# Moving the start of the weights inside their buffers: gate, up, down and the feature-major mixer units of a hybrid decoder trunk

## The chip, the cores and the metric

The kernel runs on one core of a Trainium2 chip. The metric is the device time of one execution in microseconds; each kernel is run several times and the median counts. TensorE (PE in the profile) multiplies, VectorE (DVE), ScalarE (ACT) and GpSimd (POOL) do the element-wise work, SyncE (SP) issues the loads. SBUF is the on-chip memory of 128 partitions; an address here is a byte within a partition, the same in all 128. A matmul of TensorE has two operands in SBUF: the stationary one, up to 128 x 128 numbers, which a weight load (PEld) puts into the array, and the moving one, whose columns stream through.

## What is computed

Two layers, each a half-step SwiGLU FFN, three token mixers side by side and another half-step FFN; then a final RMSNorm. 512 tokens, width 1024, FFN width 2816, everything float32.

```
for l in range(DEPTH):
    h = rms_norm(x, ffn1_norm[l])
    x = x + 0.5 * (silu(h @ wg1[l]) * (h @ wu1[l])) @ wd1[l]
    h = rms_norm(x, mix_norm[l])
    parts = split(h @ w_in[l])            # 4616 columns
    mixed = concat(hgrn2(parts), gated_deltanet(parts), retention(parts))
    x = x + mixed @ w_out[l]
    h = rms_norm(x, ffn2_norm[l])
    x = x + 0.5 * (silu(h @ wg2[l]) * (h @ wu2[l])) @ wd2[l]
return rms_norm(x, final_norm)
```

## The kernel before

**Numbers as hi and lo.** [...] To keep precision each operand is split into a rounded part hi and the rest lo, and a product is the sum of three: hi·hi, hi·lo, lo·hi (`mm3`, L217). The activations are held transposed, feature by token: eight tiles of 128 features by 512 tokens for `xh` and eight for `xl`; after the gate, `ah` and `al` per 128 columns of the FFN width.

**A unit of weights.** A unit is a block of 128 output columns with all its rows: for gate, up and the feature-major mixer columns 8 blocks of 128 x 128 (1024 numbers in a partition), for down 8 or 6 blocks. `load` (L194) brings raw weights by a DMA on SP's queue, 256 columns at a time, into one of two `raw` buffers. `split` makes the unit: ACT copies it to a `hi` tile with rounding, then DVE (or POOL, in the mixer at listed turns) subtracts to make `lo`. `unit` gives the tiles: each is a buffer of UNIT = 1088 numbers (4352 bytes, 17 x 256) in a pool of four for hi and a pool of four for lo, and the unit is laid in it from element `at` on:

```
t = pool.tile([P, UNIT], F32R, tag=tag, name=tag)
return t[:, at:at + shape[1] * shape[2]].rearrange("p (k f) -> p k f", k=shape[1])
```

`at` is 0 unless it is given. It is NARROW = 16 elements (64 bytes) in two places: the token-major mixer units, where the weights are the moving operand of 256 or 264 columns (`ps_tm`), and the last down group of the kernel, which runs in two halves of 256 tokens (`end`). Everything else begins at byte 0 of its buffer.

**Where buffers lie.** In this program's allocation the xh and xl tiles begin at byte 23296 and follow each other at 2048 bytes, the hi buffers at byte 72448 and the lo buffers at byte 89856, each 4352 bytes after the one before; the tiles that hold ah and al begin at 115456 and are 2048 apart. All of these are multiples of 256. A small pad tile (PAD = 56 elements) stands ahead of xh. A 128 x 128 block of a unit begins 512 bytes after the one before.

**The FFN.** `ffn` walks three groups of 8, 8 and 6 column blocks. For each block it runs 24 matmuls for gate (`pg`) and 24 for up (`pu`), each with a stationary 128 x 128 block of weights and 512 moving columns of `xh` or `xl`; then, after a group, eight down units (`pd`), 24 or 18 matmuls each, with `ah` or `al` moving. So gate and up take turns every 24 matmuls, and a down group is 192 or 144 matmuls long. Weights are split one unit or more ahead; the four buffers of a pool set how far. The first gate unit of the kernel is built apart, in `run`, and also begins at byte 0.

**The mixer.** `stream_units` makes the units in the order of a written plan; `dense_stream` runs the dense products and `interleave` puts the small matmuls of the mixer chains between them. Feature-major units (`ps_fm`, L260) have the weights stationary and 512 tokens moving, 24 matmuls each, as in the FFN. The output projection (`ps_out`) also streams 512 columns, from units that begin at byte 0.

Between two matmuls with different stationary blocks stands a weight load, and here every matmul has one of its own. The next load runs beside the current matmul.

Of the kernel before, what the change touches and what calls it, by code (L numbers as in the profile page):

```python
# [19 lines left out]
P = 128  # L20
D = 1024
KD = D // P
# [76 lines left out]
PAD = 56  # L99

NARROW = 16
STEP = 1600
SLICE = 2200
LAT = 1.4
# [61 lines left out]
class Kern:  # L166
# [63 lines left out]
    def stream_units(self, plan, w_out):  # L230

        for kind, cols, _ in plan:
            if kind == "fm":
                (c0, n), = cols
                raw = self.load([self.w_in[:, c0:c0 + n]], KD)
                for j in range(0, n, P):
                    yield self.split(raw[:, :, j:j + P], [P, KD, P])
            else:
                n = sum(w for _, w in cols)
                for k0 in (0, 4):  # L240
                    raw = self.load([self.w_in[:, c:c + w] for c, w in cols], 4, k0)
                    yield self.split(raw, [P, 4, n], NARROW)
        for groups in OUT_PARTS:
            n = 512 // len(groups)
            for c0 in range(0, D, n):
                raw = self.wraw.tile([P, 2 * len(groups), n], F32, tag="raw", name="raw")
                for i, g in enumerate(groups):
                    r = GROUP[g] * 256
                    self.nc.sync.dma_start(raw[:, 2 * i:2 * i + 2, :],
                                           w_out[r:r + 256, c0:c0 + n].rearrange("(k p) f -> p k f", p=P))  # L250
                yield self.split(raw, [P, 2 * len(groups), n])
# [190 lines left out]

    def gate_up(self, wg, wu, group, narrow=0, begin=(0, 0)):
        f0, nf = GROUPS[group]
        return [self.dense_units(w[:, f0 * P:(f0 + nf) * P], KD, narrow, b) for w, b in zip((wg, wu), begin)]

    def ffn(self, wg, wu, wd, layer, norm, meanwhile=None, begun=None):
        nc = self.nc
        xs = list(self.xs)
        for gi, (f0, nf) in enumerate(GROUPS):  # L450
            act, queue = [], deque()
            gu, uu = self.gate_up(wg, wu, gi) if gi or not begun else begun

            hold = 0 if gi else 2 if begun else 1
            for f in range(nf):
                where = lambda i: (self.pb, "b") if 3 <= 2 * f + i <= 2 * hold + 1 else (self.pa, "a")
                pool, tag = where(0)
                pg = pool.tile([P, T], F32, tag=tag, name="pg")
                self.mm3(pg, next(gu), xs, KD)
                if hold and f == hold:  # L460
                    self.stats_rows()
                    while queue:
                        queue.popleft()()
                pool, tag = where(1)
                pu = pool.tile([P, T], F32, tag=tag, name="pu")
                self.mm3(pu, next(uu), xs, KD)
                if hold and f == 0:
                    self.stats_tok()
                queue.append(lambda pg=pg, pu=pu: act.append(self.gated(pg, pu)))
                if f >= hold:  # L470
                    queue.popleft()()
            if gi == 0 and meanwhile:
                with self.tc.issue_after(self.last_load.ins):
                    meanwhile()
            last = gi == len(GROUPS) - 1
            if last and layer == DEPTH:
                return self.end(lambda: self.dense_units(wd[f0 * P:(f0 + nf) * P, :], nf, at=NARROW), act, nf)
            for d, dw in enumerate(self.dense_units(wd[f0 * P:(f0 + nf) * P, :], nf)):
                pd = self.pb.tile([P, T], F32, tag="b", name="pd")
                self.mm3(pd, dw, act, nf)  # L480
                nc.vector.scalar_tensor_tensor(self.x[d], pd, 0.5, self.x[d], ALU.mult, ALU.add)
                if last:
                    self.prepare(d, self.sv[layer][norm])
# [824 lines left out]
    def interleave(self, dense, waiting):  # L1308
# [3 lines left out]
        while more or any(waiting.values()) or running:  # L1312
# [5 lines left out]
            if r and (r[0] <= self.pe or not more):  # L1318
                self.pe = max(self.pe, r[0])
                self.done = self.pe  # L1320
                with self.tc.high_priority(offset=PRIO[r[1]]):
                    if next(r[2], self) is self:
                        running.remove(r)
                r[0] = max(self.done * LAT + self.pe * (1 - LAT), self.pe) + STEP
                continue
# [199 lines left out]
```

## Time and profile before

| | |
|---|---|
| median of 3 runs | 2191.91 us (2185.59 to 2193.06) |
| profiled execution | 2192.0 us, span 2190.2 us |
| TensorE busy | 2154.9 us, 98% of the span |
| weight loads busy | 1829.6 us, 84% |
| VectorE, ScalarE, GpSimd busy | 52%, 38%, 23% |
| mean granted TensorE clock | 0.992 |
| DMA | 203 MB, 93 GB/s |

Each line of the profile is the work of one core in one execution. A matmul's own duration includes its way through the array, which overlaps the next one, so the time that it costs is read from one start to the next. The chain of waits goes back from the last instruction, at each step to what released it.

### The profile page before, as it was taken

To read this page: it belongs to the slowest core of one execution; us is meant where nothing else is said; L and a number is where in the kernel's file an instruction comes from. 1 tells how busy PE (TensorE), PEld (TensorE's weight loads), DVE (VectorE), ACT (ScalarE), POOL (GpSimd) and SP (SyncE) were. 2 spreads that over 40 slices of the span, in tenths; PEclk is the share of its full clock that TensorE was granted. 3 is DMA by queue.
4 is the path that set the end of the run, shared out by engine and by line. 5 is a ranking of instruction groups with operands and counts; after the bars stand their busy time and mean duration, and the time that the engine had idled before them with its cause. 6 is when DMAs were issued, how large, how long until landed. Compare 5 with 4: busy or idle time off the path is not lost.

```text
span 2190.2 us, 31776 instructions
## 1 busy us (share of the span) xinstructions
PE 2154.9 (98%) x13079; PEld 1829.6 (84%) x13079; DVE 1147.9 (52%) x1980; ACT 842.4 (38%) x1319; POOL 500.4 (23%) x466
## 2 busy tenths in 40 slices
PE   8999999998999999999999999999899999999998
PEld 7888888887988788888888888888889888888888
DVE  5544345468497743433543343364866876434335
ACT  5322224555555422222432222254654544222225
POOL 2201013454333210101211010133633412101011
PEclk9999999999999999999999999999999999999999
DMA  4323234221123323232232322242121232323223
GB/s 155 126 78 116 77 106 140 73 78 40 59 60 106 97 97 96 78 115 80 94 116 96 97 97 96 82 148 79 59 59 40 73 103 88 104 94 99 96 87 126
DMA packets 197757, 203.08 MB, mean 93 GB/s; under 512 B 7626, under 2 KB 189292, under 8 KB 197612
## 3 DMA queue, kind: packets, MB, share of 16 engines
q1 hardware_dynamic: 197612, 201.05, 29.0%
q8 instruction: 103, 1.69, 0.3%
q14 instruction: 42, 0.34, 0.0%
HBM read 194.74 MB, written 6.29 MB: 92 GB/s over the span
## 4 chain that ended last, share of the span: by engine, by line
PE 86%; DVE 9%; ACT 2%; issue 1%; POOL 0%; DMA 0%; SPq 0%; DVEq 0%; ACTq 0%; POOLq 0%
PE pd L217 22%; PE pu L217 22%; PE pg L217 22%; PE ps_fm L260 7%; PE ps_tm L260 5%; PE ps_out L260 2%; DVE aw L149 1%; PE ps_scan L265 1%; DVE lo L149 1%; PE ps_ss L265 1%; DVE blk_p L149 1%; DVE x L149 1%; PE ps_ao L265 1%; DVE flo L149 1%; PE ps_al L265 0%
## 5 line engine op out<-in xcount | busy, mean ns | idle before, releaser
L149 ACT CAST hi<-raw 128x1024 fp32r<-128x1024 f32 (+2 forms) x369 | 379.2, 1028 | 1094.2 <-PE pg L217 323.0
L149 DVE TENSOR_TENSOR lo<-raw,hi 128x1024 fp32r<-128x1024 f32 (+2 forms) x325 | 390.2, 1201 | 80.9 <-ACT hi L149 68.5
L149 POOL TENSOR_TENSOR g<-g,rstd 128x512 f32<-128x512 f32 x88 | 150.2, 1706 | 1130.2 <-ACT g L146 1130.2
L217 PE MATMUL pd<-ah,hi 128*128 128x512 f32 (+1 forms) x752 | 282.0, 375 | 0.0
L217 PE MATMUL pd<-ah,lo 128*128 128x512 f32 (+1 forms) x752 | 281.6, 375 | 0.0
L217 PE MATMUL pd<-al,hi 128*128 128x512 f32 (+1 forms) x752 | 281.6, 375 | 0.0
L217 PE MATMUL pg<-xl,hi 128*128 128x512 f32 x704 | 275.0, 391 | 1.0 <-DVE xl L149 1.0
L217 PE MATMUL pu<-xh,hi 128*128 128x512 f32 x704 | 274.4, 390 | 0.6 <-ACT hi L149 0.6
L217 PE MATMUL pg<-xh,hi 128*128 128x512 f32 x704 | 274.5, 390 | 0.1
L217 PE MATMUL pg<-xh,lo 128*128 128x512 f32 x704 | 274.2, 389 | 0.0
L217 PE MATMUL pu<-xh,lo 128*128 128x512 f32 x704 | 274.1, 389 | 0.0
L217 PE MATMUL pu<-xl,hi 128*128 128x512 f32 x704 | 273.9, 389 | 0.0
L149 DVE TENSOR_TENSOR u<-pu,g 128x512 f32<-128x512 f32 x88 | 60.9, 692 | 280.7 <-PE pu L217 265.2
L149 DVE SCALAR_TENSOR_TENSOR x<-pd,x 128x512 f32<-128x512 f32 (+1 forms) x104 | 67.4, 649 | 229.3 <-PE pd L217 229.0
L149 DVE TENSOR_TENSOR g<-pg,rstd 128x512 f32<-128x512 f32 x88 | 60.8, 691 | 206.8 <-PE pg L217 206.7
L217 PEld LDWEIGHTS pd<-al,hi 128*128 128x128 f32 x752 | 141.4, 188 | 25.7
L217 PEld LDWEIGHTS pd<-ah,lo 128*128 128x128 f32 x752 | 141.3, 188 | 25.4
L217 PEld LDWEIGHTS pd<-ah,hi 128*128 128x128 f32 x752 | 141.1, 188 | 25.5
L217 PEld LDWEIGHTS pg<-xl,hi 128*128 128x128 f32 x704 | 132.3, 188 | 29.3 <-DVE xl L149 2.1
L217 PEld LDWEIGHTS pg<-xh,hi 128*128 128x128 f32 x704 | 132.5, 188 | 27.8 <-ACT xh L149 0.4
L217 PEld LDWEIGHTS pu<-xh,hi 128*128 128x128 f32 x704 | 132.1, 188 | 28.2 <-ACT hi L149 1.0
L217 PEld LDWEIGHTS pu<-xh,lo 128*128 128x128 f32 x704 | 132.3, 188 | 27.5
(331 smaller groups left out, 3778.5 us busy)
## 6 DMA issues: line engine op xcount, KB each, us to landing
raw<-in_ffn_w_gate_dram SPq DMA_DIRECT2D x43, 1024.0 KB, 5.1
raw<-in_ffn_w_up_dram SPq DMA_DIRECT2D x43, 1024.0 KB, 5.1
raw<-in_ffn_w_down_dram SPq DMA_DIRECT2D x32, 1024.0 KB, 4.7
raw<-in_w_in_dram SPq DMA_DIRECT2D x20, 1024.0 KB, 5.2
raw<-in_w_in_dram SPq DMA_DIRECT2D x32, 512.0 KB, 3.6
raw<-in_ffn_w_down_dram SPq DMA_DIRECT2D x20, 768.0 KB, 4.4
xd<-x SPq DMA_DIRECT2D x16, 256.0 KB, 2.5
raw<-in_w_out_dram SPq DMA_DIRECT2D x16, 256.0 KB, 2.6
```

What stands on the lines that cost most here:

```text
L149: return f(*args, **kw)
L217: self.nc.tensor.matmul(ps, a[:, k, :], b, start=n == 0, stop=n == 3 * nk - 1)
L260: self.nc.tensor.matmul(ps, a, b, start=start, stop=stop)
L265: self.nc.tensor.matmul(ps, a, b, start=start, stop=stop)
```

## The change

A table gives each kind of unit a start of its own, in elements of 4 bytes: gate 60, up 44, down 36, and the feature-major mixer units 28, that is 240, 176, 144 and 112 bytes. `gate_up`, `ffn` and `stream_units` pass it on to `dense_units` and `split`, and so to `unit`. Sizes of tiles and pools, loads, engines, the order of the work and the number of instructions stay. The token-major units, the last down group of the kernel, the output projection's units and the very first gate unit keep their starts. What moves is the address that ACT, DVE and POOL write, that DVE and POOL read hi from, and that TensorE loads the weights from.

```diff
+WIDE = {"gate": 60, "up": 44, "down": 36, "mix": 28}
...
                 raw = self.load([self.w_in[:, c0:c0 + n]], KD)
                 for j in range(0, n, P):
-                    yield self.split(raw[:, :, j:j + P], [P, KD, P])
+                    yield self.split(raw[:, :, j:j + P], [P, KD, P], WIDE["mix"])
...
     def gate_up(self, wg, wu, group, narrow=0, begin=(0, 0)):
         f0, nf = GROUPS[group]
-        return [self.dense_units(w[:, f0 * P:(f0 + nf) * P], KD, narrow, b) for w, b in zip((wg, wu), begin)]
+        return [self.dense_units(w[:, f0 * P:(f0 + nf) * P], KD, narrow, b, WIDE[n])
+                for w, b, n in zip((wg, wu), begin, ("gate", "up"))]
...
-            for d, dw in enumerate(self.dense_units(wd[f0 * P:(f0 + nf) * P, :], nf)):
+            for d, dw in enumerate(self.dense_units(wd[f0 * P:(f0 + nf) * P, :], nf, at=WIDE["down"])):
```

## The prediction

> **What bounds the kernel now.** First the page: busy time by engine, and the chain that ended last.
>
> ```profile
> span 2190.2 us, 31776 instructions
> PE 2154.9 (98%) x13079; PEld 1829.6 (84%) x13079; DVE 1147.9 (52%) x1980; ACT 842.4 (38%) x1319; POOL 500.4 (23%) x466
> ...
> PE pd L217 22%; PE pu L217 22%; PE pg L217 22%; PE ps_fm L260 7%; PE ps_tm L260 5%; PE ps_out L260 2%; DVE aw L149 1%; PE ps_scan L265 1%; DVE lo L149 1%; PE ps_ss L265 1%; DVE blk_p L149 1%; DVE x L149 1%; PE ps_ao L265 1%; DVE flo L149 1%; PE ps_al L265 0%
> ```
>
> TensorE carries the chain: the three FFN products take two thirds of it, the feature-major mixer product `ps_fm` 7%. The next view is the chain in order of time (start, length, what), then the busy time of each engine in a gate/up stage and in a down stage (length; busy time and count of PE, PEld, DVE, ACT, POOL; granted clock; DMA share; GB/s).
>
> ```profile
> 48.71 5.44 PE pg L217 x24
> 54.15 5.44 PE pu L217 x24
> ...
> 234.18 43.52 PE pd L217 x192
> ...
> 342.98 32.64 PE pd L217 x144
> ```
> ```profile
> 147.14:234.18 87.04, 87.04 (x385) 72.07 (x385) 34.80 (x39) 26.32 (x33) 13.90 (x8) 1.00 0.32 103
> 234.18:277.70 43.52, 43.52 (x193) 36.04 (x193) 15.94 (x17) 9.03 (x10) 0.00 (x0) 1.00 0.26 86
> ```
>
> The reader is to see a rigid beat. A unit of 24 matmuls takes 5.44 us, 192 take 43.52 and 144 take 32.64: each time 226.67 ns from one start to the next, at a granted clock of 1.00, with no wait between units. Only something that changes this beat can move the FFNs, because weights arrive early (DVE is 40% busy, ACT 30%, DMA 32%).
>
> How many matmuls does the edit touch? The groups by form of TensorE, one of three alike for each product (hi·hi, hi·lo, lo·hi), and one weight load:
>
> ```profile
> L217 PE MATMUL pg<-xh,hi 128*128 128x512 f32 x704 | 274.5, 390 | 0.1
> L217 PE MATMUL pu<-xl,hi 128*128 128x512 f32 x704 | 273.9, 389 | 0.0
> L217 PE MATMUL pd<-al,hi 128*128 128x512 f32 x656 | 254.7, 389 | 0.0
> L260 PE MATMUL ps_fm<-xl,hi 128*128 128x512 f32 x320 | 128.8, 403 | 0.0
> L260 PE MATMUL ps_out<-mh,lo 128*128 128x512 f32 x128 | 50.5, 394 | 0.0
> L217 PE MATMUL pd<-al,hi 128*128 128x256 f32 x96 | 26.9, 281 | 0.0
> L217 PEld LDWEIGHTS pg<-xh,lo 128*128 128x128 f32 x704 | 132.3, 188 | 27.0
> ```
>
> A matmul's own duration (389 ns) is longer than the beat because consecutive ones overlap; I use start-to-start times alone. Touched are 3 x 704 for gate less the first unit's 24 (it is built apart and keeps byte 0), 3 x 704 for up, 3 x 656 for down: 2088 + 2112 + 1968 = 6168 in the FFNs; and 3 x 320 = 960 `ps_fm`. `ps_out` stays at byte 0, the 256-wide down product stays at 64 bytes. All touched weights are the stationary operand of a 512-column stream; the streamed operand does not move.
>
> **The change part by part.** It adds and removes no instruction, no wait, no DMA and no buffer; it moves where ACT and DVE (or POOL) write a unit's hi and lo and where TensorE loads them from.
>
> *Writers.* No tile of the trace begins off a 64-byte step, so the nearest rows are the casts of 768 columns: at byte 0 (first row, a window around the first last-group of down) and at byte 64 (second row, a window at the end of the kernel):
>
> ```profile
> L149 ACT CAST hi<-raw 128x768 fp32r<-128x768 f32 x5 | 4.2, 840 | 12.1 <-PE pd L217 7.2 <-PE pu L217 3.8 <-ACT xh L149 0.9
> ```
> ```profile
> L149 ACT CAST hi<-raw 128x768 fp32r<-128x768 f32 x13 | 10.7, 830 | 10.8 <-PE pu L217 3.8 <-PE pd L217 3.6 <-DMA raw<-in_ffn_w_down_dram 3.3
> ```
>
> 840 and 830 ns: no penalty. I take zero; were a cast a tenth longer, ACT would still be under 35% busy in the stage above. The cover is the 5.44 us that TensorE spends on the unit before; gone, each ns would count once per unit.
>
> *TensorE.* 512 columns cost 226.67 ns. Is that the stream alone, or does the weight load that runs beside it hold it up? The trace has two witnesses. First, the 256-wide token-major product (`ps_tm`), as a timeline (start, length, instruction) in two stretches of the same line, operand tiles and start offsets, and ahead of it the busy times there (TensorE first; the granted clock is the third number from the end).
>
> ```profile
> 472.00:490.00 18.00, 15.58 (x129) 13.91 (x131) 17.59 (x40) 9.92 (x17) 11.79 (x19) 1.00 0.19 60
> ...
> 652.00:653.50 1.50, 1.50 (x15) 1.50 (x15) 1.47 (x3) 1.38 (x3) 0.31 (x1) 1.00 0.43 146
> ```
> ```profile
> 471.96 0.28 PE L260 MATMUL ps_tm<-hi,xh 128*128 128x256 f32 x1
> ...
> 476.20 0.28 PE L260 MATMUL ps_tm<-hi,xh 128*128 128x256 f32 x1
> ```
> ```profile
> 652.06 0.28 PE L260 MATMUL ps_tm<-hi,xh 128*128 128x256 f32 x1
> ...
> 654.22 0.28 PE L260 MATMUL ps_tm<-hi,xl 128*128 128x256 f32 x1
> ```
>
> The clock is 1.00 in both. The first stretch makes 36 steps in 4.24 us, 117.8 ns each; the second 19 steps in 2.16 us, 113.7 ns. One instruction form has two beats, 4.1 ns apart, and each holds until something interrupts it. Second witness, the wide product after an interruption (the 0.5 us of `ps_ms` ahead of it):
>
> ```profile
> 31.26 0.40 PE L217 MATMUL pu<-xh,hi 128*128 128x512 f32 x1
> ...
> 33.34 0.39 PE L217 MATMUL pu<-xh,hi 128*128 128x512 f32 x1
> ...
> 36.74 0.39 PE L217 MATMUL pg<-xh,hi 128*128 128x512 f32 x1
> ```
>
> Nine steps in 2.08 us are 231.1 ns each; the next fifteen in 3.40 us are 226.7. So the step depends on how the stream and the load beside it stand to each other in time, and it settles. I read this as two readers of the same memory that sometimes want the same part of it. If so, the place where the weights begin relative to the stream (both at multiples of 256 bytes today) is a second way to set that relation, and the edit turns it by 240, 176, 144 or 112 bytes, all odd multiples of 16, which no row shows.
>
> The price per wide matmul is therefore bounded from both sides. Best: the whole excess goes. The slower narrow beat and the wide one differ by 226.67 - 117.8 = 108.9 ns for 256 columns, so 512 columns with no fixed part would take 217.7 ns, 9.0 below today. Worst: the unsettled 231.1 ns stays, 4.4 above. Between them I take the one step that the trace shows between two settled beats of one form, 4.1 ns down, since a shifted start is most like a shifted phase.
>
> The rule in the Trainium skill that speaks against this is in "TensorE: Matmul & The Clock Gate", section "Step-by-step: what each phase is for": the stream and LDWEIGHTS have independent SBUF read ports, and loading the next weights doesn't take bandwidth from the running matmul. By it the sum would be zero and the time 2192; it does not account for 113.7 beside 117.8. The same page's section "Wait — 56ns, not 53.3ns?" gives 215.7 ns for back-to-back matmuls of 512 columns; by that figure 11 ns per matmul could go at most, an estimate of 2114 us.
>
> *The sum.* FFNs: every touched matmul is on the chain, 6168 x 4.1 = 25.3 us. `ps_fm`: 960 x 226.67 = 218 us of streaming, of which the chain holds 7% of 2190 = 153 us, so 70% of 960 x 4.1 = 3.9 counts, 2.8 us. Together 28 us. The profiled execution took 2192.0 us with a span of 2190.2, and the median of the runs shown is 2191.91, the same within 0.1 us: 2192 - 28 = **2164 us**. What is late next? Nothing: at 222.6 ns a unit takes 5.34 us, against some 2.2 us of DVE per unit (34.80 / 16).
>
> **The rivals.**
>
> *The beat is the stream's own.* 226.67 ns is what 512 columns of this type cost, and the load has room beside it (188 of 227 ns). For it: no gap in 192 matmuls, and hi and lo in all eight weight buffers, against xh, xl, ah and al, give one beat. It also settles from an interruption, so it may settle on the same beat from any start address. Against it: the two narrow beats. Time: 2192, within 0.3%.
>
> *All the excess goes.* 9.0 ns: 6168 x 9.0 + 0.7 x 960 x 9.0 = 61.6 us, 2130 us. [...] Against: the better narrow beat, 113.7 ns, is still 4.8 above half of 217.7.
>
> *It never stays settled.* Gate and up take turns every 24 matmuls, and with 240 and 176 bytes their loads no longer stand alike to the stream. Place: the first matmuls of each unit. Price: nine steps at 4.4 ns, 40 ns a unit; with 88 gate and 88 up units 7 us, 2199. If the new places never let it settle, 4.4 x (6168 + 0.7 x 960) = 30 us, 2222. It decides from the point where a unit's loss at its start exceeds what it gains in the rest: 40 ns are 1.7 ns per matmul of 24. For it: the nine slow steps above. Against: down, whose offset stays for the 144 or 192 matmuls of a group, would be free of the swap, and a third of the wide matmuls with it.
>
> **How the numbers follow.** A measurement of this kernel can tell about 0.3%, 6.6 us, from no change. Forecast, some 4 ns per matmul: 0.31, with a range of its own of 2150 to 2178. All the excess: 0.15. No change: 0.30. Never settled: 0.24. Faster is the first two, 0.46; same 0.30; slower 0.24. The range runs from 2120 (a little under the full gain) to 2210 (two thirds of the full loss); what lies above that and below 2120 is about 2 in 10 with the misses inside a case.
>
> **What would show it.** Right: units of gate, up and down in the chain at 5.34 us (x24) instead of 5.44, down groups at 42.7 instead of 43.52, the same counts, the same clock of 1.00, `ps_out` at its old beat, casts of 768 columns at 830 to 840 ns. No change: 5.44 and 43.52 again. Never settled: units of 5.48 to 5.55, with the first nine steps longer than the rest. The argument falls if the beat of gate, up and down moves by different amounts with their different offsets, or if ACT or DVE, not TensorE, show the difference.

## The result, and the profile after

The changed kernel takes 2217.82 us (median of 5, 2216.59 to 2217.96) against 2191.91 us: a ratio of 1.0127, 95% interval 1.0111 to 1.0143. It is 26 us slower where 28 us less were forecast, and it lies above the range. The page of the changed kernel (lines of its file stand one lower) shows the same instructions and the same bytes moved (203 MB), but TensorE busy 26.6 us longer:

```profile
span 2215.6 us, 31776 instructions
PE 2181.5 (98%) x13079; PEld 1828.6 (83%) x13079; DVE 1145.3 (52%) x1980; ACT 841.0 (38%) x1319; POOL 499.5 (23%) x466
```

The chain in order of time (start, length, what) shows where they come from:

```profile
160.85 5.48 PE pg L218 x24
166.33 5.52 PE pu L218 x24
...
237.85 44.81 PE pd L218 x192
282.66 5.44 PE pg L218 x24
288.11 5.53 PE pu L218 x24
...
348.57 33.60 PE pd L218 x144
```

A gate unit takes 5.44 to 5.49 us, an up unit 5.51 to 5.53, a down group 44.81 and 33.60, where a settled unit took 5.44 and the groups 43.52 and 32.64. As beats, from one start to the next: gate 226.7 to 228.7 ns, up 230.0, down 233.3, all against 226.67. Nothing waits in between, and the granted clock is 1.00 as before, as the busy times of a gate/up and a down stage show (columns as in the prediction):

```profile
150.00:237.80 87.80, 87.80 (x385) 71.88 (x384) 34.68 (x39) 26.06 (x33) 13.89 (x8) 1.00 0.31 100
237.90:282.60 44.70, 44.70 (x193) 35.96 (x192) 15.94 (x17) 8.89 (x10) 0.00 (x0) 1.00 0.26 85
```

Added up over the stages, from the first matmul of one to the first of the next, gate and up take 971.0 us before and 981.2 after, down 485.1 and 498.2, the two mixers 717.1 and 719.0: 10.2 + 13.1 + 1.9 = 25.2 of the 25.4 us by which the spans differ.

The mixers need care, because their clock differs between executions. In them the trace has stretches of about 3.4 us at a granted clock of 0.50 (half clock), ten before and nine after (one of 6.8 us counts as two); one of before is

```profile
439.50:442.90 3.40, 3.40 (x10) 2.66 (x9) 1.43 (x9) 0.00 (x0) 0.00 (x0) 0.50 0.52 150
```

Runs below whose mixer units begin at byte 0 take 715.9 us in the mixers with nine such stretches (down alone), 716.6 to 717.5 with ten, 719.9 with twelve (the added matmuls at byte 0). Like with like, the mixers of the change are thus about 3.1 us slower, not 1.9; their feature-major matmuls settle on 233.3 ns as well.

The writers are as fast as before. A cast of 768 columns (a down unit of six blocks, now at 144 bytes; fp32r is the type of the hi tiles) takes 834 ns in a window around the first last-group of down:

```profile
L150 ACT CAST hi<-raw 128x768 fp32r<-128x768 f32 x6 | 5.0, 834 | 16.6 <-PE pd L218 7.7 <-PE pu L218 3.9 <-PE pg L218 3.9
```

### The profile page after: what moved, and what is told of

Its sections match the earlier page's. It is cut to its first block, busy times and chain, and to the rows that moved or that the text cites. A ratio compares the mean times of both kernels' runs of the same rounds, so it can differ in the third digit from the quotient of the medians.

```text
span 2215.6 us, 31776 instructions
## 1 busy us (share of the span) xinstructions
PE 2181.5 (98%) x13079; PEld 1828.6 (83%) x13079; DVE 1145.3 (52%) x1980; ACT 841.0 (38%) x1319; POOL 499.5 (23%) x466
## 4 chain that ended last, share of the span: by engine, by line
PE 89%; DVE 8%; ACT 1%; issue 1%; POOL 0%; DMA 0%; SPq 0%; DVEq 0%; ACTq 0%; POOLq 0%
PE pd L218 22%; PE pu L218 22%; PE pg L218 22%; PE ps_fm L261 8%; PE ps_tm L261 6%; PE ps_out L261 2%; DVE aw L150 1%; PE ps_scan L266 1%; DVE lo L150 1%; PE ps_ss L266 1%; DVE x L150 1%; PE ps_ao L266 1%; PE ps_al L266 0%; PE ps_co L266 0%; DVE blk_p L150 0%
## 5 line engine op out<-in xcount | busy, mean ns | idle before, releaser
L218 PEld LDWEIGHTS pu<-xl,hi 128*128 128x128 f32 x704 | 132.1, 188 | 29.6
```

Source lines behind the costliest of these rows:

```text
L218: self.nc.tensor.matmul(ps, a[:, k, :], b, start=n == 0, stop=n == 3 * nk - 1)
```

## Experiments

All of them start from the changed kernel and set starts anew. "Beat" is the mean from one matmul's start to the next. Theory A: weight load and moving stream collide, and the difference of their starts counts. Theory B: only the alignment of the weights counts. Theory C: the alternation of gate and up counts. Theory H was formed after the first eight runs.

### Twenty-four starts, in two sweeps

```diff
-WIDE = {"gate": 60, "up": 44, "down": 36, "mix": 28}
+WIDE = {"mix": 0}
+GU = [0, 4, 8, 12, 16, 20, 24, 28, 32, 36, 40, 44]
+DN = [0, 4, 8, 12, 16, 20, 24, 28, 32, 36, 40, 0]
...
-        return [self.dense_units(w[:, f0 * P:(f0 + nf) * P], KD, narrow, b, WIDE[n])
-                for w, b, n in zip((wg, wu), begin, ("gate", "up"))]
+        return [self.dense_units(w[:, f0 * P:(f0 + nf) * P], KD, narrow, b, GU[3 * self.nffn + group])
+                for w, b in zip((wg, wu), begin)]
```

> Every FFN group gets its own start, the same for its gate and up units, and each down group its own: gate/up groups 1 to 12 at 0, 16, 32, 48, 64, 80, 96, 112, 128, 144, 160, 176 bytes, down groups 1 to 11 at 0, 16, ... 160 bytes; mixer units at 0. Nothing is left out. Theory A (the weight load and the moving stream contend, and what counts is the weights' start less the stream's start, modulo 256): a beat that is constant within a group and depends on the start in a graded way: 226.7 ns at 0, about 230 at 176, about 233 at 112 and 144. Theory B (the load's own alignment: how many rows of memory a block of 512 bytes touches): a step, every start that is not a multiple of 64 or 128 costs the same, multiples of it cost nothing. Theory C (the swap: gate and up at different starts unsettle each other, as the prediction's third rival had it): 226.7 ns everywhere, since gate and up stand alike within a group.

> As the first sweep with the remaining starts: gate/up groups 1 to 12 at 192, 208, 224, 240, 4, 8, 12, 24, 40, 56, 120, 248 bytes, down groups 1 to 11 at 176, 192, 208, 224, 240, 4, 8, 12, 24, 56, 120 bytes; mixer units at 32 bytes. Nothing is left out. Theory A: graded, coming back to 226.7 ns as the start nears 256 (228 to 229 at 240), starts below 16 bytes within 2 ns of 226.7. Theory B: 192 as cheap as 0; all others like 112, near 233. Theory C: 226.7 everywhere.

One execution each took 2224.21 and 2218.34 us, beside 2191.36 for the kernel before. The beats in ns, gate/up and down, by start in bytes; each value is one group's, entered from the group ahead of it:

| start | gate/up | down | | start | gate/up | down |
|---|---|---|---|---|---|---|
| 0 | 226.7 | 226.7 | | 80 | 232.0 | 232.0 |
| 4 | 232.4 | 232.4 | | 96 | 234.3 | 234.3 |
| 8 | 230.7 | 230.7 | | 112, 128, 144, 160 | 233.0 to 233.3 | 233.3 |
| 12 | 233.3 | 230.0 | | 120 | 226.7 | 226.7 |
| 16 | 226.7 | 226.7 | | 176 | 230.0 | 230.0 |
| 24 | 230.0 | 230.0 | | 192 | 229.0 to 229.5 | 229.0 |
| 32, 48, 56, 64 | 233.3 | 233.3 | | 208 | 231.8 | 231.9 |
| 40, 248 | 233.3 | not run | | 224 | 233.3 | 233.3 |
| | | | | 240 | 226.9 to 227.0 | 226.7 |

Chain lines of the first sweep: the down group at 0, one at 16, the one at 32 (144 matmuls), then those at 48 and 64 bytes:

```profile
104.03 43.60 PE pd L221 x192
...
234.67 43.53 PE pd L221 x192
...
345.40 33.60 PE pd L221 x144
...
830.83 44.79 PE pd L221 x192
...
965.23 44.80 PE pd L221 x192
```

The start sets the beat, with gate and up at the same start too, so C falls. It is neither graded by distance, as A had it, nor a step, as B had it. No start is faster than byte 0; 16, 120 and 240 are as fast here, and eleven cost about 6.6 ns. At 12 bytes gate/up and down differ with one and the same start: the first sign that the start isn't all. The slow values hold for a group as it was entered here; runs below find a faster beat at 144 bytes.

### Stream and weights shifted together, and apart

```diff
-PAD = 56
+PAD = 28
...
-WIDE = {"gate": 60, "up": 44, "down": 36, "mix": 28}
+WIDE = {"gate": 0, "up": 0, "down": 0, "mix": 0}
...
+            self.pad2 = pool("pad2", 1)
+            self.pad2.tile([P, 28], F32, name="pad2")
             self.wraw = pool("wraw", 2)
```

The second pad tile is in the second kernel alone. The built programs lay tiles at multiples of 32 bytes, so the shift came out otherwise than the expectations say: in the first kernel x, weights, ah and al all begin 160 bytes into a row of 256; in the second x at 160, the weights and ah and al at 32, so weights and x are 128 apart.

> All units back at byte 0 of their buffers, but the pad tile ahead of xh is 112 bytes shorter, so that x, raw weights, weights and the tiles of ah and al all begin 112 bytes lower and no longer at multiples of 256. Nothing is left out. Theory A: gate, up, down and the feature-major units stay at 226.7 ns, time as before within 0.3%, since weights and stream stand to each other as before. Theory B: near 233 ns for all of them, some 45 us slower than before.

> All units at byte 0 of their buffers, at multiples of 256; only xh and xl begin 112 bytes lower. Nothing is left out. Theory A: gate, up and the feature-major units, whose stream moved, go to about 233 ns, down (stream of ah and al, not moved) stays at 226.7; about 4200 matmuls by 6.6 ns and the feature-major part, some 30 us slower than before. Theory B: 226.7 ns everywhere, time as before.

One execution each: 2188.73 and 2215.19 us, beside 2191.36 before. Chain lines, first of the kernel with everything shifted, then of the one with x and weights apart:

```profile
152.49 5.44 PE pu L218 x24
157.93 5.44 PE pg L218 x24
...
234.09 43.52 PE pd L218 x192
```
```profile
154.35 5.60 PE pu L218 x24
159.95 5.60 PE pg L218 x24
...
238.35 43.53 PE pd L218 x192
```

Weights 160 bytes off cost nothing when the stream is 160 off too; with weights 128 bytes from x, gate and up take 233.3 ns (5.60 / 24), while down, whose stream moved with them, keeps 226.7. B falls. What counts is where the load stands to the stream: that half of A holds.

### Half a weight load

```diff
-                self.nc.tensor.matmul(ps, a[:, k, :], b, start=n == 0, stop=n == 3 * nk - 1)
+                m = P if n == 0 or n == 3 * nk - 1 or nk < KD else P // 2
+                self.nc.tensor.matmul(ps[0:m], a[:, k, 0:m], b, start=n == 0, stop=n == 3 * nk - 1)
```

> All units at byte 0. In gate, up and the down groups of 8 blocks, every matmul of a unit but its first and last loads only 64 of the 128 columns of weights and still streams 512 columns; so the upper half of the output rows misses 22 of 24 products, a part of the computation that is left out. Down groups of 6 blocks keep full loads. Theory A1 (even at equal starts the load holds the stream up): the excess over the streaming floor of 217.7 ns (9 ns) shrinks with the load by about half, some 222 ns. Theory A2 (at equal starts nothing collides any more, 226.7 ns is what the stream costs by itself): 226.7 ns also with half a load.

> The same half loads, with all units at 144 bytes (the same part of the computation is left out). If the 6.7 ns by which 144 bytes cost more than 0 come from collisions of the load with the stream, half a load has fewer: 228 to 231 ns in gate, up and the down groups of 8, and 233.3 still in the down groups of 6 with full loads. If they are a fixed cost of a shifted start per matmul, 233.3 everywhere.

Chain lines at byte 0, then at 144 bytes:

```profile
154.70 5.51 PE pu L219 x24
160.21 5.51 PE pg L219 x24
...
237.40 44.11 PE pd L219 x192
```
```profile
155.17 5.59 PE pu L219 x24
160.75 5.59 PE pg L219 x24
...
238.97 43.71 PE pd L219 x192
298.99 5.44 PE pu L219 x24
...
347.95 32.64 PE pd L219 x144
```

At byte 0 the units with half loads are slower than whole ones, 229.7 ns, and at 144 bytes they run on two beats, about 233 in the early units of each FFN and 226.7 in the later ones; the down groups of 6, which have full loads, run at 226.7 there (32.64 / 144). Both expectations missed: neither 222 nor 226.7 came at byte 0, and 226.7 was not foreseen at 144. Two things follow: fewer columns to load do not bring the beat below 226.7 (A1 falls), and one start can have two beats. Why a unit that mixes half and whole loads is slower at byte 0 is not shown.

### Up at gate's start

```diff
-WIDE = {"gate": 60, "up": 44, "down": 36, "mix": 28}
+WIDE = {"gate": 60, "up": 60, "down": 36, "mix": 28}
```

> The change with up at 240 bytes, as gate, instead of 176; gate 240, down 144, mixer 112 as in the change. Nothing is left out. Theory A with settling (the beat that a start settles on depends also on how the stream stood before it): up goes from 230.1 to 226.8 ns, and gate, whose start is unchanged, from 228.5 to 226.8, since nothing unsettles it; 2112 x 5.1 = 10.8 us less than the changed kernel, about 2207 us, ratio to before near 1.007. Without settling: gate stays at 228.5, about 2211 us.

2201.64 us, ratio 1.0056 (1.0038 to 1.0074). The interval holds the 1.007 that was expected, but the parts differ. Gate, not touched by this edit, goes to 227.1 ns on the mean like up, and the gate/up stages give back 8.6 us (972.6 in all). Down, not touched either, gives back 9.3 (488.9), which was not expected: eight of its eleven wide groups run at 226.67. The mixers took 4.1 us more, with twelve stretches at half clock instead of nine. In the chain:

```profile
98.14 5.48 PE pu L218 x24
...
104.05 44.83 PE pd L218 x192
...
230.48 5.44 PE pu L218 x24
235.92 43.52 PE pd L218 x192
...
344.72 32.64 PE pd L218 x144
...
823.48 5.48 PE pu L218 x24
828.96 44.81 PE pd L218 x192
```

The mean hides two beats at 240 bytes: 228.4 ns (units of 5.48 us) in the first group of the first, second and fourth FFN, and 226.7 (5.44) in the others once settled. The three down groups at 233.3 ns are those that follow units of 5.48 us; the eight at 226.67 follow units of 5.44.

### Down alone

```diff
-WIDE = {"gate": 60, "up": 44, "down": 36, "mix": 28}
+WIDE = {"gate": 0, "up": 0, "down": 36, "mix": 0}
```

> One part alone: down units at 144 bytes, gate, up and mixer units at byte 0. Nothing is left out. Theory A: down at 233.3 ns, gate and up at 226.7 after a few matmuls, 1968 x 6.67 = 13.1 us more than before, ratio near 1.006. If the cost of the change lay in the alternation of gate and up: no change.

The expected 13 us did not come: ratio 1.0009 (1.0000 to 1.0019). The first down group has the slow beat, the ten others, at the same start, the fast one:

```profile
103.04 0.43 PE ps_sv L1361 x2
103.47 44.82 PE pd L218 x192
...
235.34 43.52 PE pd L218 x192
...
344.14 32.64 PE pd L218 x144
```

What sets the first group apart is `ps_sv`, two small matmuls of the setup (a transpose), that stand directly before it. From this came theory H: a start allows one or more settled beats; 144 bytes allow 226.7 and 233.3; and a group keeps the beat on which it is entered. The down groups of the run before, at 233.3 ns behind units of 5.48 us and at 226.67 behind units of 5.44, fit it too. Up at 176 bytes, which has about 230.0 in every run with that start, would then be what throws gate and down off the fast beat in the changed kernel.

### Up and down, gate and mixer at byte 0

```diff
-WIDE = {"gate": 60, "up": 44, "down": 36, "mix": 28}
+WIDE = {"gate": 0, "up": 44, "down": 36, "mix": 0}
```

> Gate and mixer units at byte 0; up at 176 and down at 144 bytes as in the change. Nothing is left out. Theory H (history: a start allows one or more settled beats; 176 allows only the slow 230.0, 144 allows 226.7 and 233.3 and keeps the one that it is entered on; a group entered from up at 176 is entered off the fast beat): all eleven wide down groups at 233.3, although ten of them ran at 226.7 with the same start when up stood at byte 0; up 230.0, gate back to 226.7 after a few matmuls. 2112 x 3.4 + 1968 x 6.67 = 20 us more than before, ratio near 1.009. Without history: down at 226.7 but for the first group, as in the run with down alone; 7 + 1.3 us, ratio near 1.004.

2211.33 us, ratio 1.0097 (1.0080 to 1.0114), with 1.009 expected. All eleven wide down groups have 233.3 ns, though their start is that of the run before; gate at byte 0 pays a few slow matmuls per unit (5.45 us here, 227.4 ns on the mean of all):

```profile
153.87 5.52 PE pu L218 x24
159.39 5.45 PE pg L218 x24
...
236.21 44.80 PE pd L218 x192
```

### A small matmul ahead of each down group

```diff
+            kick = self.pb.tile([P, 64], F32, tag="b", name="kick")
+            nc.tensor.matmul(kick, self.c("ident"), self.ones_d, start=True, stop=True)
             for d, dw in enumerate(self.dense_units(wd[f0 * P:(f0 + nf) * P, :], nf, at=WIDE["down"])):
```

> Down alone at 144 bytes, and one small added matmul (128 x 128 stationary, 64 columns, its result unused) ahead of each down group. It stands directly before the first down matmul in 8 of 11 wide groups; in three (the first group of the second, third and fourth FFN) it comes out ahead of a gate unit instead. Nothing is left out. Theory H: the 8 groups at 233.3 ns, the three others at 226.7; 1200 matmuls more on the slow beat than with down alone, 8.0 us, and some 0.3 us for each added matmul. If the entry doesn't matter: the first group at 233.3 as before, the others 226.7.

> The control: the same added matmuls, all units at byte 0. Nothing is left out. Theory H with byte 0 allowing one settled beat alone: every down group at 226.7 after some nine matmuls, time as before but for some 0.3 us per added matmul. If an interruption alone leaves a slow beat behind: 233 here too.

Chain lines with down at 144 bytes, then with everything at byte 0:

```profile
235.75 0.17 PE kick L481 x2
235.92 44.86 PE pd L218 x192
```
```profile
235.01 0.17 PE kick L481 x2
235.18 43.58 PE pd L218 x192
```

With down at 144 bytes the eight groups that directly follow an added matmul have 233.3 ns to their last matmul, and the three others 226.7; with byte 0 all have 226.7 after at most three steps. The down stages take 495.0 and 485.7 us, 9.2 apart (8.0 were expected for the seven groups that changed, and the first group, slow already in the run with down alone, adds 1.3). One interruption of 0.17 us costs the group behind it 1.28 us at 144 bytes and nothing lasting at byte 0. The whole executions, one each, took 2203.46 and 2198.01 us beside 2189.24; their mixers differ by 3 us the other way, with ten stretches at half clock against twelve.

### The narrow matmuls

```diff
+TM = [16, 0, 4, 8, 12, 20, 24, 28, 16, 32, 36, 40, 44, 48, 56, 60]
...
-                    yield self.split(raw, [P, 4, n], NARROW)
+                    yield self.split(raw, [P, 4, n], at)
```

> All stationary weights at byte 0; the token-major units, whose weights are the moving operand of 256 columns, begin at a start of their own per part: in the first layer 64 (264 wide), then 0, 16, 32, 48, 80, 96, 112 bytes, in the second layer 64, then 128, 144, 160, 176, 192, 224, 240 bytes. Nothing is left out. Theory A: the beat of the narrow matmuls also depends on the stream's start less the load's; some starts hold the 113.4 ns beat throughout, others 117.7 or more; the mixer stage moves by at most 5 us. If the two narrow beats come from the interruptions alone: the same mixture of 113 and 118 at every start.

One execution took 2186.80 us. The beats of the 256-wide matmuls spread over 113 to 126 ns, with means by start of 116 (112 bytes) to 120 (96 bytes). Before, at 64 bytes throughout, the same parts have means of 115.6 to 117.8, so the place in the mixer accounts for some of the spread; 120 is beyond it, which speaks for the start, but no start holds 113 throughout. Left open. The time is no gain either: the mixers have six stretches at half clock here and ten before. No run points to a version that is clearly faster than the kernel before.

## Why the prediction was wrong

**What bounds the kernel** was right: the loss follows the beat of the wide matmuls. 23.3 of the 25.4 us are longer steps of gate, up and down, with the same counts, a clock of 1.00 and no waits. The mixers' share was taken at 2.8 us per 4.1 ns, which makes 4.5 at 6.67 ns; about 3.1 were found.

**The parts that cost nothing** were right: casts at 834 ns, DVE and POOL no longer busy than before. (Not every tile of the kernel before begins on a 64-byte step, as the prediction says; one small raw tile of the mixer begins 32 bytes off it. The sum does not need it.)

**That the place of the weights relative to the stream is a second way to set the step** was right, and the kernels with shifted tiles show it: 226.7 ns with weights and stream both at 160 bytes, 233.3 with 128 between them.

**The step that failed** is the value between the bounds, "I take the one step that the trace shows between two settled beats of one form, 4.1 ns down". The sign was taken from the narrow matmuls, as if the wide ones stood on the slower of their beats. They stand on the fastest that was found: of 24 starts none is below 226.67 ns, and the change moved gate, up and down by +1.5, +3.3 and +6.7 ns. Different amounts for different starts were the prediction's own sign that its argument falls.

The two narrow beats were no evidence on the start either, since both occur at one start. The last down group of the kernel, always at 64 bytes, has 117.8 ns a step before and after the change and 113.3 in the run with up and down (23.32 and 22.44 us for 198 matmuls); first before, then that run:

```profile
2144.35 23.32 PE pd L217 x198
```
```profile
2164.69 22.44 PE pd L218 x198
```

The nine slow steps showed only that byte 0 comes back to 226.67, not whether another start is better or worse. (The `ps_ms` ahead of them took 0.84 us, not 0.5, with two gate matmuls in between.)

**The upper bound** failed too. 231.1 ns, the mean of the nine unsettled steps, was taken for the worst; settled beats of 233.3 and 234.3 exist. The range ended at 2210 besides, below the 2222 of its own rival. With 6.67 ns in place of 4.4 the same sum gives 6168 x 6.67 + 0.7 x 960 x 6.67 = 46 us as the worst case, 2238 us, and 2218 lies inside.

**The rivals.** That the beat is the stream's own and doesn't move is refuted for the step as a whole, but its floor held: 226.67 ns is the fastest settled beat that any start or half a load gave. That all the excess goes is refuted. The third, never settled, had the right side and nearly the right size (2222), with a mechanism that is half right; the size is partly luck, since one 4.4 ns for every matmul stands there for 1.5, 3.3 and 6.7. Gate and up at 240 and 176 bytes do disturb each other: with up at gate's start, gate and up both ran at 227.1 ns. The unit lengths that it named, 5.48 to 5.55 us, are nearly those measured (5.44 to 5.53). Its place, the first steps of a unit, holds for gate alone and in four of its twelve groups (239, 232 and 229 ns, then 226.7). In the other eight gate repeats steps of about 229, 229, 229 and 226 ns, and up repeats 226, 229, 236 and 229 from its first matmul to its last. And down, which I held to be free of the swap, pays most, 13.1 us, because it is entered off the fast beat and at 144 bytes does not return to it.

**The rule of the Trainium skill** that was weighed there ("TensorE: Matmul & The Clock Gate", section "Step-by-step: what each phase is for": the stream and LDWEIGHTS have independent read ports, and a load doesn't take bandwidth from the running matmul) does not account for these matmuls. The same instructions take 226.7 or 233.3 ns with the load elsewhere. Its time, 2192, was nearer than the forecast all the same. (The 11 ns per matmul that the prediction weighs beside it come to 2117 us with the mixer at 70%, as in the sum, not 2114.)

**What stays open** is the cause beneath: which part of the memory or of TensorE's path the two reads share, why 16, 120 and 240 bytes are like 0 and 8 is not, and what carries the beat from one unit into the next. That load and stream collide is argued from the dependence on their difference; half a load did not cost half, so a simple count of collisions is not shown. Each slow value of the table was entered in one way only; whether those starts have a faster beat, as 144 bytes have, is open too.

## What to carry to other kernels

Where every matmul streams 512 float32 columns and loads new weights, measure the step from start to start by group: starts of tiles within a row of 256 bytes can cost 3% of it, and weights and stream that begin alike were the safe choice here, because with whole loads that place came back to the fast beat after every interruption. A place that is as fast in one run may have a second, slow beat, on which a single small matmul or a neighbour with another start leaves it; so test a layout with the interruptions that the kernel has. That a beat is reached again from slower steps does not tell which beat it is: down at 144 bytes also comes from steps of 239, 235 and 240 ns and settles on 233.3, the slow one of its two.

## What the runs showed that was not expected

- Two settled beats at one start: 226.67 and 233.3 ns at 144 bytes (44.82 and 43.52 us for 192 matmuls within one execution), each kept to the end of the group where the loads are whole.
- The dependence on the start is jagged: 4 bytes cost 5.7 ns, 8 bytes 4.0, 16 bytes nothing.
- A start costs others more than itself: up at 176 bytes loses 3.3 ns on its own 2112 matmuls, 7 us; the eleven wide down groups at 144 bytes lose 1.2 us with up at byte 0 and 13.0 with up at 176 (446.2 us before, 447.4 and 459.3).
- Loading half as many weight columns in 22 of a unit's 24 matmuls made the step longer at byte 0, 229.7 instead of 226.7 ns.
- The granted clock halves for some 3.4 us at a time in the mixers, six to twelve times an execution, and the mixers' time goes with it: 715.9 us with nine, 719.9 with twelve, both with mixer units at byte 0.
